# Spread products of the maxima, split inputs stored by GpSimd, values stored by tokens: a transformer layer on one Trainium2 core

## The chip, the cores and the metric

The kernel runs on one core of a Trainium2 chip. The core has a matrix engine (TensorE, "PE"), a vector engine (VectorE, "DVE"), a scalar engine (ScalarE, "ACT"), a general engine (GpSimd, "POOL") and a sync engine ("SP") which here only issues transfers. Each engine works through its own list of instructions in order; semaphores hold an instruction until its inputs are there and its output's memory is free. Transfers (DMAs) between DRAM and the on-chip memory are issued by SP, ACT and POOL into a queue of their own each and are carried by 16 DMA engines that all queues share. The metric is the time of one execution in device microseconds (us).

## The reference

One layer on 2048 tokens (S) of width 1024 (D), all in float32: attention with forget gates in 8 heads of 64, beside it a gated MLP over chunks of 128 positions, an output projection of both, and a feed-forward part.

```python
xn = rms_norm(x, mix_norm_g[l])
h = xn @ w_in[l]
q, k, v, f_logit, z = jnp.split(h, [D_ATTN, 2 * D_ATTN, 3 * D_ATTN, 3 * D_ATTN + N_ATTN_HEADS], axis=-1)
...
log_f = jax.nn.log_sigmoid(f_logit.astype(jnp.float32) + b_f[l].astype(jnp.float32))
attn = forgetting_attention(q, k, v, log_f)   # softmax(q.k/8 + c[t] - c[s], s <= t) @ v, c = cumsum(log_f)
sgu = spatial_gating(jax.nn.gelu(z, approximate=False), sgu_ln_g[l], sgu_ln_b[l], w_s[l], b_s[l])
merged = jnp.concatenate([rms_norm(attn, out_norm_g[l, :D_ATTN]), rms_norm(sgu, out_norm_g[l, D_ATTN:])], axis=-1)
x = x + merged @ w_out[l]
xn = rms_norm(x, ffn_norm_g[l])
gate, up = jnp.split(xn @ w_gate_up[l], 2, axis=-1)
x = x + (jax.nn.silu(gate) * up) @ w_down[l]
...
return rms_norm(x, final_norm_g)
```

## The kernel before, in words

**Split numbers.** PE multiplies in a shortened float format. Each operand is therefore split into a high part and a low part (names end in `h` and `l`: `xh`, `xl`, `wh`, `wl`), and a product takes three matmuls: high by high, high by low, low by high. L123 (ACT) makes a high part and L126 (DVE) a low one; both are helpers that all stages use.

**Projections (chunks).** The tokens go by in four chunks c = 0 to 3 of 512. For each chunk PE makes the logits of the forget gates (L526), then eight groups of 24 matmuls for queries and keys (L552: `which` = 0 is Q, 1 is K, `pr` is a pair of heads), then four groups of 24 for the values V (L447); chunk 0 has its V groups first. The split inputs of a chunk (`xh`, `xl`, two blocks of 128 features in each tile) are kept for later: `keep` (L266 to L269) writes them to the DRAM tensor `XS`, in the order [128, 4 token blocks, high/low, 8 feature blocks, 128 tokens], with four SP transfers of 256 KB for each pair, called after the stores of the low part of Q or K. Q and K go to DRAM as `QH`, `QL`, `KH`, `KL`, and the values (`v_close`, L447 to L461) as `VD`, in the order [head, token, 129], by ACT's queue or, for chunk 0 and the last two V groups of chunk 3, SP's.

**Maxima.** The softmax needs for each query the largest score over the keys. These are made from the high parts alone by extra matmuls: `one_max` (L354 to L363) multiplies 128 queries (a slice of tile `A`) with 512 keys (tile `D`) into a PSUM tile `mx_ps`, of which there are two, and DVE reduces it (L359, or L362 for the block on the diagonal). `max_stream` walks over the heads of a chunk and yields after each product; at the end of a head `turn` (L374 to L379) transposes the maxima and stores them (`md`). In the projections the maxima of chunk c−1 are run during chunk c (generator `early`): `between(n_early, ...)`, called after each group, takes the next `n_early` steps in one go (3, 6 and 7 for chunks 1, 2, 3, from the table `EB`), after one step of the forget gates (`gates_`, L310 to L350: the row of gates goes out to DRAM by ACT's queue, comes back by POOL's as `F`, and is then worked through by ACT, DVE and PE) and one step of loading the next chunk (`xg`). The remaining maxima are made during attention.

**Attention and z.** After the last V group come, interleaved on PE, the scores (L714, L715), the exponentials on ACT (L717), their split (L123, L126), the causal mask on POOL (L727) and the products with V (L747, L749, L752), and the z projection (L872) which reads the split inputs back from `XS`, one block of 128 tokens at a time: 32 tiles of 1 MB each. The first is loaded by SP into `wsth` and `wstl` (at the end of the projections); the other 31 (`xz`, two buffers) by POOL's queue (L865). Keys, queries and values (`D`, `C`, `A`, `B`, `V`) are loaded by SP.

**Output projection and feed-forward.** Each tile t of 128 tokens, once projected, goes through `out_done` (L1097 to L1116): the sum of squares on ACT, the reciprocal root `r3` in two steps (L172 on DVE, L174 on POOL), the scaling on DVE (L1106, `xn`, or `xb` for the last tile), and transposes on PE (L1113). It is a generator, and the caller takes one step of it between pieces of other work. The feed-forward part (L1614) starts on the result; its weights are added on POOL and DVE (L1303) and split.

**What sets the order.** The framework places each instruction by the order in which the code issues it and by its own estimate of when its inputs are ready; `behind(...)` (issue_after) holds everything inside until the named instructions have been placed. So the order on each engine is fixed when the program is built.

## Time and profile before

| | |
|---|---|
| median of 3 runs | 2403.47 us (2403.11 to 2408.91) |
| profiled execution | 2400.57 us |
| its span | 2398.9 us |
| DMA | 372.22 MB, mean 155 GB/s |
| HBM read, written | 249.15 MB, 120.98 MB |
| V stores by ACT's queue, chunks 1 to 3 (60 to 345 us) | 10 of 516 KB |
| stores of the split inputs by SP's queue (60 to 345 us) | 64 of 256 KB |

The profile was taken in one execution; times within it are counted from the start of the span. A row of the timeline names start, duration, engine, line, operation and tiles, and in brackets how long the engine stood idle just before and what it waited for. PE takes a matmul of 512 columns about every 0.23 us although each lasts 0.39, since they overlap. The stages are: projections from 0 to 345 us, attention with z from there to about 900, the output projection to about 1128, the feed-forward part to the end.

### The profile page before, as it was taken

To read this page: it belongs to the slowest core of one execution; us is meant where nothing else is said; L and a number is where in the kernel's file an instruction comes from. 1 tells how busy PE (TensorE), PEld (TensorE's weight loads), DVE (VectorE), ACT (ScalarE), POOL (GpSimd) and SP (SyncE) were. 2 spreads that over 40 slices of the span, in tenths; PEclk is the share of its full clock that TensorE was granted. 3 is DMA by queue.
4 is the path that set the end of the run, shared out by engine and by line. 5 is a ranking of instruction groups with operands and counts; after the bars stand their busy time and mean duration, and the time that the engine had idled before them with its cause. 6 is when DMAs were issued, how large, how long until landed. Compare 5 with 4: busy or idle time off the path is not lost. (4 is left out here: it accounts for less than half of the span.)

```text
span 2398.9 us, 31422 instructions
## 1 busy us (share of the span) xinstructions
PE 2344.1 (98%) x10582; PEld 1893.2 (79%) x10582; DVE 1668.5 (70%) x2736; ACT 1057.5 (44%) x1770; POOL 636.0 (27%) x704
## 2 busy tenths in 40 slices
PE   9999989999999999999999999999999999999998
PEld 7778767777777767877888888788888878888886
DVE  6658658888887676566656555965556587696888
ACT  5322127777777776444333332433333242332433
POOL 1000011222212232221323232422323244454431
PEclk9999999999999999999999999999999999999999
DMA  9856776555576655665333323433232344555453
GB/s 257 269 155 207 189 197 196 164 156 164 172 214 191 197 167 162 206 209 171 118 89 87 97 71 88 131 98 88 80 96 72 88 135 172 176 193 193 144 202 147
DMA packets 338632, 372.22 MB, mean 155 GB/s; under 512 B 22612, under 2 KB 259860, under 8 KB 332456
## 3 DMA queue, kind: packets, MB, share of 16 engines
q1 hardware_dynamic: 313672, 311.24, 42.9%
q0 software_dynamic: 7472, 43.06, 5.4%
q10 hardware_dynamic: 17328, 15.91, 2.3%
q8 instruction: 85, 1.39, 0.2%
q14 instruction: 75, 0.61, 0.1%
HBM read 249.15 MB, written 120.98 MB: 154 GB/s over the span
## 5 line engine op out<-in xcount | busy, mean ns | idle before, releaser
L123 ACT CAST wh<-raw 128x512 fp32r<-128x512 f32 (+2 forms) x492 | 302.1, 621 | 745.2 <-PE pp L1614 622.9
L126 DVE TENSOR_TENSOR wl<-raw,wh 128x512 fp32r<-128x512 f32 (+2 forms) x496 | 375.5, 767 | 83.8 <-ACT wh L123 83.3
L1614 PE MATMUL pp<-wl,wh 128*128 128x512 f32 x1056 | 325.3, 389 | 1.9 <-ACT u L1414 1.0
L1614 PE MATMUL pp<-wh,wh 128*128 128x512 f32 x1056 | 325.0, 389 | 0.0
L1303 POOL TENSOR_TENSOR raw<-raw 128x512 f32<-128x512 f32 (+1 forms) x124 | 171.1, 1381 | 524.6 <-DMA raw<-in_w_gu_dram 361.1
L126 DVE TENSOR_TENSOR Pl<-Pt,Ph 128x512 fp32r<-128x512 f32 (+1 forms) x320 | 195.9, 617 | 81.0 <-ACT Ph L123 76.3
L1614 PEld LDWEIGHTS pp<-wl,wh 128*128 128x128 f32 x1056 | 198.0, 188 | 43.7 <-ACT u L1414 1.4
L1614 PEld LDWEIGHTS pp<-wh,wh 128*128 128x128 f32 x1056 | 198.2, 188 | 41.1
L717 ACT ACTIVATE Pt<-mx_ps 128x512 f32<-128x512 f32 (+1 forms) x320 | 169.2, 533 | 124.9 <-PE mx_ps L715 119.5
L1614 PE MATMUL pp<-wl,wl 128*128 128x512 f32 x528 | 205.7, 390 | 1.0 <-DVE wl L126 0.9
L1614 PE MATMUL pp<-wh,wl 128*128 128x512 f32 x528 | 205.4, 389 | 0.0
L872 PE MATMUL z<-wh,xz 128*128 128x512 f32 x496 | 188.9, 396 | 0.0
L1303 DVE TENSOR_TENSOR raw<-raw,raw 128x512 f32<-128x512 f32 (+1 forms) x112 | 131.9, 1180 | 78.4 <-POOL raw L1303 74.9
L123 ACT CAST Ph<-Pt 128x512 fp32r<-128x512 f32 (+1 forms) x320 | 176.1, 556 | 20.8 <-PE tp L749 5.9
L359 DVE TENSOR_REDUCE mx<-mx_ps 128x1 f32<-128x512 f32 x192 | 129.8, 682 | 18.7 <-PE mx_ps L357 17.9
L747 PE MATMUL tp<-Ph,V 128*128 128x512 f32 (+1 forms) x320 | 119.1, 372 | 6.1 <-POOL Ph L727 4.5
L357 PE MATMUL mx_ps<-D,A 66*128 66x512 f32 (+2 forms) x320 | 116.7, 380 | 8.2 <-DVE mx L359 4.2
L752 PE MATMUL tp<-Pl,V 128*128 128x512 f32 (+1 forms) x320 | 119.4, 373 | 3.4 <-DVE Pl L126 2.7
L714 PE MATMUL mx_ps<-A,D 74*128 74x512 f32 (+1 forms) x320 | 119.6, 374 | 0.9 <-DMA A<-md 0.6
L715 PE MATMUL mx_ps<-B,C 128*128 128x512 f32 (+1 forms) x320 | 118.1, 369 | 0.0
L1614 PEld LDWEIGHTS pp<-wl,wl 128*128 128x128 f32 x528 | 99.1, 188 | 22.6 <-DVE wl L126 2.1
L1614 PEld LDWEIGHTS pp<-wh,wl 128*128 128x128 f32 x528 | 99.1, 188 | 20.6
(341 smaller groups left out, 5259.8 us busy)
## 6 DMA issues: line engine op xcount, KB each, us to landing
raw<-in_w_gu_dram SPq DMA_DIRECT2D x88, 512.0 KB
xz<-XS POOLq DMA_DIRECT2D x31, 1024.0 KB, 5.6
HD<-hT SPq DMA_DIRECT2D x44, 512.0 KB
D<-KH SPq DMA_DIRECT2D x112, 128.0 KB
XA<-xa SPq DMA_DIRECT2D x27, 512.0 KB
raw<-HD SPq DMA_DIRECT2D x24, 512.0 KB
XA<-xb SPq DMA_DIRECT2D x21, 512.0 KB
xa<-XA SPq DMA_DIRECT2D x20, 512.0 KB
```

Of the source, the lines that this page charges most:

```text
L123: return nc.scalar.copy(o, i) if eng is nc.scalar else eng.tensor_copy(o, i)
L126: return eng.tensor_tensor(o, i, f(h), ALU.subtract)
L357: nc.tensor.matmul(pm[:, 0:n], lhs, Dt[0 : lhs.shape[0], 0:n], start=True, stop=True)
L359: nc.vector.tensor_reduce(mx[:, a, s : s + 1], pm, AX.X, ALU.max)
L714: nc.tensor.matmul(st[:, off:], Dt[:, b * P : (b + 1) * P], A[:, off:], start=True, stop=False)
L715: nc.tensor.matmul(st[:, off:], C[:, b * P : (b + 1) * P], B[:, off:], start=False, stop=True)
L717: nc.scalar.activation(Pt[:, off:], st[:, off:], AF.Exp)
L747: nc.tensor.matmul(pv[:, off:], V[:, 0:P], Ph[:, off:], start=kb == 0, stop=False)
L752: nc.tensor.matmul(pv[:, off:], V[:, 0:P], Pl[:, off:], start=False, stop=kb == 4 * j + 3)
L872: nc.tensor.matmul(pz, xz[a][:, k, :], w[b][:, k, :], start=n == 0, stop=n == 3 * KT - 1)
L1303: (nc.vector if e == "v" else nc.gpsimd).tensor_tensor(o, a, b, op)
L1614: nc.tensor.matmul(pm, a[:, k, :], b[:, k, :], start=on is None and k == 0 and e == 0, stop=k == it.kh - 1 and e == 2, skip_group_check=n ...
```

## The change

1. `EB` for the last chunk is 12 in place of 10, so `n_early` there is 6 in place of 7. The steps of the maxima are no longer taken after a group: inside a group, ahead of the three matmuls of each feature block k, `maxima(n, k)` takes its even share of them, and holds the three matmuls behind the last maxima product that stood two calls earlier. So the maxima lie between the main products of all groups, Q, K and V.
2. `keep` stores each tile with one transfer of 512 KB on POOL's queue, with a dependency (`pace`) on the low part of Q or K of the same pair of heads; `XS` is laid out [128, high/low, 8, 512 tokens], so that a store writes runs of 4096 bytes and a load of 128 tokens reads runs of 512 bytes (before: the other way round, 512 and 8192).
3. `VD` is laid out [token, head, 129]: a store writes 4128 bytes in one run per token (before 516); a load still reads runs of 516 bytes.
4. The 31 `xz` loads are issued by SP in place of POOL; the load of the first two (`wsth`, `wstl`) reads the new layout.
5. In `out_done` the last two tiles (t = 14, 15) no longer stop between sum of squares, reciprocal root and scaling.

Numbers of instructions on PE, DVE and ACT stay; SP loses 64 stores and gains 31 loads; POOL gains 32 stores and loses 31 loads.

```diff
-EB = [1, 12, 12, 10]
+EB = [1, 12, 12, 12]
...
+    def pace(a, b):
+
+        tc.add_manual_dep(a.ins, b.ins.name, mybir.DependencyInfo(mybir.DependencyClass.Sync, mybir.DependencyReason.DATA),
+                          reason="pace")
...
-    XS = [T(dram, [P, 4, 2, KT, P], F32R, f"XS{c}") for c in range(NCH)]
+    XS = [T(dram, [P, 2, KT, CH], F32R, f"XS{c}") for c in range(NCH)]
...
-    VD = [T(dram, [H, CH, P + 1], F32R, f"VD{c}") for c in range(NCH)]
+    VD = [T(dram, [CH, H, P + 1], F32R, f"VD{c}") for c in range(NCH)]
...
-        def keep(self, i):
+        def keep(self, i, by):
             for a, t in enumerate((self.hi[i], self.lo[i])):
-                for m in range(2):
-                    s = ldr(XS[self.c][:, :, a, 2 * i + m, :], t[:, m].rearrange("p (t q) -> p t q", t=4))
+                pace(nc.gpsimd.dma_start(f(XS[self.c][:, a, 2 * i : 2 * i + 2, :]), f(t)), by)
...
-        nc.tensor.matmul(pm[:, 0:n], lhs, Dt[0 : lhs.shape[0], 0:n], start=True, stop=True)
+        last_mx.append(nc.tensor.matmul(pm[:, 0:n], lhs, Dt[0 : lhs.shape[0], 0:n], start=True, stop=True))
...
-    def between(n, *done):
+    def between(*done):
         with behind(*done):
             next(gates_, None)
             next(xg, None)
-        for _ in range(n):
+
+    def maxima(n, k):
+
+        marks.append(last_mx[-1:])
+        for _ in range((k + 1) * n // KT - k * n // KT):
             next(early, None)
+        return marks[0]
+
+    marks = deque([[], []], maxlen=3)
...
-        s = queue(xc.c if xc.c < NCH - 1 or tt < 2 else 0).dma_start(f(VD[xc.c][:, tt * P : (tt + 1) * P, :].rearrange("h p d -> p h d")), f(v))
+        s = queue(xc.c if xc.c < NCH - 1 or tt < 2 else 0).dma_start(f(VD[xc.c][tt * P : (tt + 1) * P]), f(v))
...
-                    for a, b in ((lh, rh), (lh, rl), (ll, rh)):
-                        mm = nc.tensor.matmul(pm, a, b, start=n == 0, stop=n == 3 * KT - 1)
-                        n += 1
+                    with behind(*maxima(n_early, k)):
+                        for a, b in ((lh, rh), (lh, rl), (ll, rh)):
+                            mm = nc.tensor.matmul(pm, a, b, start=n == 0, stop=n == 3 * KT - 1)
+                            n += 1
...
-                    with behind(s):
-                        xc.keep(pr)
+                    xc.keep(pr, b)
...
-                between(n_early, a, b, mm)
+                between(a, b, mm)
...
-            v_part(pm, xc, tt, range(KT))
+            for k in range(KT):
+                with behind(*maxima(n_early, k)):
+                    v_part(pm, xc, tt, [k])
...
-            between(n_early, a, b)
+            between(a, b)
...
-                nc.gpsimd.dma_start(f(xz.rearrange("p a k t -> p (a k t)")),
-                                    f(XS[q][:, cc].rearrange("p a k t -> p (a k t)")))
+                ldr(xz.rearrange("p a k t -> p (a k) t"),
+                    XS[q][:, :, :, cc * P : (cc + 1) * P].rearrange("p a k t -> p (a k) t"))
...
-        yield
+        if t < NB - 2:
+            yield
         r = rsqrt(pev, ss, 1.0 / D, "r3")
-        yield
+        if t < NB - 2:
+            yield
...
-        xz_in = [ldr(xz0[a], XS[0][:, 0, a]) for a in range(2)]
+        xz_in = [ldr(xz0[a], XS[0][:, a, :, 0:P]) for a in range(2)]
```

How this moves instructions is shown at three places.

PE, end of the third and start of the fourth V group of chunk 3, before (`mm` are the main products of V, `mx_ps` products for the maxima; numbers behind a name tell one tile from another):

```order
L447 MATMUL mm_3314<-wvh_273,xh_1714 128x512
L357 MATMUL mx_ps_3203<-D_3075,A_3050 128x512
L447 MATMUL mm_3314<-wvl_274,xh_1714 128x512
L447 MATMUL mm_3314<-wvh_273,xl_1718 128x512
L357 MATMUL mx_ps_3206<-D_3075,A_3050 128x512
L447 MATMUL mm_3314<-wvh_273,xh_1714 128x512
L447 MATMUL mm_3314<-wvl_274,xh_1714 128x512
L357 MATMUL mx_ps_3209<-D_3075,A_3050 128x512
L447 MATMUL mm_3314<-wvh_273,xl_1718 128x512
L447 MATMUL mm_3345<-wvh_273,xh_1711 128x512
L357 MATMUL mx_ps_3212<-D_3075,A_3050 128x512
L447 MATMUL mm_3345<-wvl_274,xh_1711 128x512
```

PE, end of the second V group and start of the third, after (line numbers of the changed file; L460 was L447, L363 was L357, L729 and L730 were L714 and L715):

```order
L363 MATMUL mx_ps_3243<-D_3104,A_3022 128x384
L460 MATMUL mm_3210<-wvh_273,xh_1698 128x512
L460 MATMUL mm_3210<-wvl_274,xh_1698 128x512
L460 MATMUL mm_3210<-wvh_273,xl_1702 128x512
L363 MATMUL mx_ps_3250<-D_3104,A_3022 128x512
L460 MATMUL mm_3210<-wvh_273,xh_1698 128x512
L460 MATMUL mm_3210<-wvl_274,xh_1698 128x512
L460 MATMUL mm_3210<-wvh_273,xl_1702 128x512
L460 MATMUL mm_3271<-wvh_273,xh_1695 128x512
L729 MATMUL mx_ps_3454<-A_3429,D_867_3414 128x512
L730 MATMUL mx_ps_3454<-B_3432,C_862_3409 128x512
L460 MATMUL mm_3271<-wvl_274,xh_1695 128x512
```

Before, a maximum stands behind every second matmul far into the fourth V group; after, the last maximum stands at the end of the second group, and the third and fourth hold first scores of attention in place of maxima. From that last maximum to the first z matmul there are 75 instructions; the first z stood directly behind the last V matmul and stands 18 instructions behind it now.

SP, end of the projections, before (`VD<-v` is the store of the third V group, `wsth` and `wstl` the first inputs of z, `KL` a store of a low part of K, `md` a store of maxima):

```order
L120 DMA C_865_3444<-KL_3_62_125 64x512
L120 DMA D_870_3449<-KH_3_46_109 64x512
L458 DMA VD_78_141<-v_3339 128x8x129
L120 DMA wsth_3429<-XS_7_70 128x1024
L120 DMA wstl_3430<-XS_7_70 128x1024
L120 DMA md_2_837_3273<-mr_3271 8x128
```

and after (L125 was L120, L471 was L458):

```order
L125 DMA KL_3_74_137<-ql_3139 128x512
L125 DMA md_2_818_3182<-mr_3180 8x128
L125 DMA D_870_3417<-KH_3_46_109 64x512
L125 DMA wsth_3397<-XS_7_70 128x8x128
L125 DMA wstl_3398<-XS_7_70 128x8x128
L125 DMA md_2_845_3287<-mr_3285 8x128
L471 DMA VD_78_141<-v_3307 128x1032
```

The two loads stood behind the store of V, now they stand ahead of it.

DVE, end of the output projection, before (`wl` and `wh` are weights of the feed-forward part, `r3a` the first step of the reciprocal root of the last tile, `xb` its scaling):

```order
L126 TENSOR_TENSOR wh_12290<-sg_3072_11568,wh_12290 128x2048
L126 TENSOR_TENSOR wl_12303<-raw_3201_12213,wh_12302 128x512
L126 TENSOR_TENSOR wl_12315<-raw_3199_12209,wh_12314 128x512
L126 TENSOR_TENSOR wl_12319<-raw_3201_12213,wh_12318 128x512
L126 TENSOR_TENSOR wl_12367<-raw_3200_12211,wh_12366 128x512
L1303 TENSOR_TENSOR raw_3199_12209<-raw_3200_12211,raw_3199_12209 128x512
L1303 TENSOR_TENSOR raw_3201_12213<-raw_12215,raw_3201_12213 128x512
L126 TENSOR_TENSOR wl_12373<-raw_12215,wh_12372 128x512
L172 TENSOR_SCALAR r3a_12402<-ss_3213_12286 128x1
L126 TENSOR_TENSOR wl_12438<-raw_3199_12209,wh_12437 128x512
L1106 SCALAR_TENSOR_TENSOR xb_12285<-xa_12055,r3r_12404,ffb_10109 128x1024
```

and after (L131 was L126, L177 was L172, L1123 was L1106, L1320 was L1303):

```order
L131 TENSOR_TENSOR wh_12279<-sg_3072_11536,wh_12279 128x2048
L177 TENSOR_SCALAR r3a_12272<-ss_3217_12270 128x1
L131 TENSOR_TENSOR wl_12292<-raw_3201_12181,wh_12291 128x512
L1123 SCALAR_TENSOR_TENSOR xb_12269<-xa_12023,r3r_12274,ffb_10077 128x1024
L131 TENSOR_TENSOR wl_12304<-raw_3199_12177,wh_12303 128x512
L131 TENSOR_TENSOR wl_12308<-raw_3201_12181,wh_12307 128x512
L131 TENSOR_TENSOR wl_12340<-raw_3200_12179,wh_12339 128x512
L1320 TENSOR_TENSOR raw_3199_12177<-raw_3200_12179,raw_3199_12177 128x512
L1320 TENSOR_TENSOR raw_3201_12181<-raw_12183,raw_3201_12181 128x512
L131 TENSOR_TENSOR wl_12346<-raw_12183,wh_12345 128x512
```

`r3a` stood behind seven weight instructions and stands directly behind the split of `sg` now; `xb` stands six rows earlier. On POOL, the second step `r3r` stood behind two adds of `raw` and stands ahead of them.

## The prediction, made before the changed kernel had run

> **What bounds the kernel now.** I read the page first, then busy time by stages, then TensorE's (PE) waits, then the timeline around the three places where it stands still.

> ```profile
> span 2398.9 us, 31422 instructions
> PE 2344.1 (98%) x10582; PEld 1893.2 (79%) x10582; DVE 1668.5 (70%) x2736; ACT 1057.5 (44%) x1770; POOL 636.0 (27%) x704
> ```

> PE works for 2344.1 of 2398.9 us. The change removes none of its matmuls, so only PE's idle 54.8 us and the time lost to a lowered clock can be won. The next view gives busy time by stage (columns: window, length, then busy us and instruction count by engine, then granted clock, DMA share, GB/s).

> ```profile
> core 0: us, PE busy (x) PEld busy (x) DVE busy (x) ACT busy (x) POOL busy (x), PEclk, DMA share, GB/s
> 95.00:345.00 250.00, 242.25 (x1092) 191.96 (x1091) 169.98 (x474) 60.56 (x86) 7.94 (x17) 0.99 0.71 195
> 345.00:360.00 15.00, 10.16 (x35) 7.47 (x34) 3.80 (x10) 5.34 (x12) 3.31 (x10) 0.77 0.73 183
> 360.00:620.00 260.00, 256.38 (x1214) 200.33 (x1214) 216.92 (x430) 190.39 (x337) 58.34 (x134) 1.00 0.57 170
> 620.00:885.00 265.00, 259.15 (x1234) 200.42 (x1233) 204.67 (x396) 208.88 (x387) 66.90 (x147) 1.00 0.60 185
> 1128.00:1136.00 8.00, 4.74 (x26) 3.77 (x25) 5.51 (x7) 2.83 (x5) 2.23 (x3) 1.00 0.49 186
> 1136.00:2399.00 1263.00, 1245.14 (x5483) 1027.90 (x5481) 860.41 (x1101) 427.41 (x686) 431.79 (x291) 1.00 0.39 122
> ```

> Length less busy time is PE's idle time: 7.75 us in chunks 1 to 3 of the projections, 4.84 us in the 15 us where these give way to attention, 3.62 and 5.85 us in the two halves of attention, 3.26 us where the output projection gives way to the feed-forward part, and 17.86 us in that part, which the change doesn't touch. Finer windows find the first two, and the clock:

> ```profile
> 98.00:126.00 28.00, 25.65 (x118) 20.45 (x117) 22.90 (x67) 14.12 (x20) 0.11 (x1) 1.00 0.95 281
> 176.00:186.00 10.00, 9.56 (x43) 7.29 (x42) 8.59 (x23) 5.99 (x9) 0.11 (x1) 1.00 0.63 192
> 264.00:275.00 11.00, 8.46 (x39) 6.64 (x38) 8.04 (x20) 4.20 (x7) 0.65 (x1) 1.00 0.58 170
> 325.00:335.00 10.00, 7.58 (x30) 5.62 (x29) 3.07 (x7) 2.18 (x3) 0.14 (x1) 0.93 1.08 229
> 335.00:345.00 10.00, 10.00 (x43) 8.07 (x42) 6.55 (x20) 0.69 (x1) 0.00 (x0) 0.90 0.57 122
> 345.00:355.00 10.00, 5.16 (x16) 3.74 (x15) 2.23 (x7) 3.38 (x8) 0.54 (x2) 0.78 0.76 167
> 355.00:365.00 10.00, 10.00 (x43) 7.42 (x42) 6.53 (x12) 5.66 (x10) 2.77 (x8) 0.88 0.85 278
> ```

> Four places hold all of the first 7.75 us: 2.35 + 0.44 + 2.54 + 2.42. Ten times what the clock lacks of 1.00 is the time lost to it in a 10-us row: 0.7 + 1.0 = 1.7 us around 335, 2.2 + 1.2 = 3.4 us behind 345. So at most 7.75 + 1.7 + 4.84 + 3.4 + 3.26 = 20.95 us can be won at the places that the change is near, outside of attention. What PE waits for there (us, times, longest):

> ```profile
> PE mx_ps L357 <- DVE mx L359: 4.2, 3, 2.5
> PE tp L331 <- DVE v L327: 2.6, 1, 2.6
> PE z L872 <- DMA wsth<-XS: 4.3, 1, 4.3
> PE tp L1113 <- DVE xb L1106: 3.3, 1, 3.3
> ```

> **The change part by part.**

> *Maxima spread between the main products.* No instruction is added on PE or VectorE (DVE); the order changes. A product for the maxima needs one of two banks, which DVE frees with its reduction (L359, L362). Where several stand close together in PE's order and DVE is late, PE stops. That is so in the V groups of chunk 3:

> ```profile
> 331.41 0.39 PE L447 MATMUL mm<-wvh,xl 128*128 128x512 f32 x1
> 333.01 0.50 PE L357 MATMUL mx_ps<-D,A 66*128 66x512 f32 x1 [1.21 <-DVE mx L359]
> 333.35 0.45 PE L447 MATMUL mm<-wvh,xh 128*128 128x512 f32 x1
> 333.59 0.63 PE L447 MATMUL mm<-wvl,xh 128*128 128x512 f32 x1
> 334.02 0.63 PE L357 MATMUL mx_ps<-D,A 66*128 66x512 f32 x1
> ```

> ```profile
> DVE v L456 <- DMA VD<-v: 7.5, 1, 7.5
> ```

> DVE stood 7.5 us at v's low part, because v's buffer was still being stored, and the maxima behind it stood with it. In the new order the dense stretch is gone and the third and fourth V group hold no maximum at all, so a late DVE holds nobody there. I count the places at 98, 176 and 325, with the clock that fell at the last, as won: 2.35 + 0.44 + 2.42 + 1.7 = 6.9 us. At 264 something else is late:

> ```profile
> 268.76 0.23 DVE L321 TENSOR_SCALAR v<-v 128x128 f32<-128x128 f32 x1 [2.96 <-issue]
> ```

> DVE idles for 2.96 us ahead of the forget gates, whose row comes back from DRAM behind the V stores; these become shorter (below), but the chain stays. I take half of 2.54, 1.3 us, between 0 and 2.54. Part sum −8.2 us, bounds 0 and −9.45.

> What it may cost: every main product now stays behind maxima of two calls before, so PE can't run ahead of a full DVE. How full DVE is:

> ```profile
> 185.00:215.00 30.00, 30.00 (x143) 24.61 (x142) 27.98 (x73) 11.45 (x16) 0.00 (x0) 1.00 0.83 250
> ```

> 93% in chunk 2, and PE lost nothing here; the row at 176 lost 0.44 us beside DVE at 86%. At worst each of about six such groups waits for one reduction of about 0.7 us: 4 us; at best 0. Six times 0.44 would be 2.6; I take 1.5 us, nearer to the row of 185 to 215.

> *The inputs' split tiles stored by GpSimd (POOL), V by tokens.* Sixty-four stores of 256 KB leave SP's queue, 32 of 512 KB enter POOL's. POOL is busy for 7.94 of 250 us here, so its issues have room; each waits for a low part, and behind it stand the next chunk's forget row and r, due a chunk later. SP's queue is what is relieved: D, KL and QL no longer stand behind stores. I give this no term of its own: it is why the first part's gains should hold. Bounds −1 and +2 us, the +2 if r or the forget row behind a held store comes late.

> *The first z loads.* At the seam PE goes from V directly to z, whose first input lands late:

> ```profile
> 345.13 0.39 PE L447 MATMUL mm<-wvh,xl 128*128 128x512 f32 x1
> 349.86 0.47 PE L872 MATMUL z<-wh,wsth 128*128 128x512 f32 x1 [4.34 <-DMA wsth<-XS]
> ```

> ```profile
> 340.34 0.39 SPq L458 DMA_DIRECT2D VD<-v  x1
> 340.83 0.53 SPq L120 DMA_DIRECT2D wsth<-XS  x1
> 341.41 1.12 SPq L120 DMA_DIRECT2D wstl<-XS  x1
> ```

> wsth leaves 0.5 us behind the V store for which SP held still, and lands 9 us after its issue (340.83 to 349.86). In the new order both loads stand ahead of that store; wstl's memory is free once the last maximum is done, which is 75 PE instructions, about 75 × 0.23 = 17 us (the step of PE's rows above), ahead of the first z. 9 us fit into 17. The wait and the clock behind it go: 4.84 + 3.4 = −8.2 us. What is late next: 18 scores and P-times-V products now stand ahead of the first z, and the later of these wait for exp, split and mask of scores that stand some 2 us ahead of them; I give back 1 us, between 0 and 3. Part sum −7.2 us, bounds 0 and −8.2.

> *Two steps less in the last tiles' norm.*

> ```profile
> 1124.49 2.49 DVE L126 TENSOR_TENSOR wl<-raw,wh 128x512 fp32r<-128x512 f32 x4
> 1131.04 0.14 DVE L172 TENSOR_SCALAR r3a<-ss 128x1 f32<-128x1 f32 x1
> 1132.23 1.28 DVE L1106 SCALAR_TENSOR_TENSOR xb<-xa,r3r,ffb 128x1024 f32<-128x1024 f32 x1 [0.44 <-POOL r3r L174]
> 1125.91 3.46 POOL L1303 TENSOR_TENSOR raw<-raw 128x512 f32<-128x512 f32 x2 [9.86 <-DVE wl L126]
> ```

> r3a moves ahead of the four splits at 1124.49 and r3r ahead of POOL's two adds, so xb can start near 1127 instead of 1132.23, and PE's 3.26 us go. In turn the adds start about 2 us later, and the last weight split behind them comes later by that, some 0.7 us more than its cover: −3.3 + 0.7 = −2.6 us, bounds −3.3 and 0.

> *The 31 later z loads go from POOL's queue to SP's*, in 512-byte pieces.

> ```profile
> xz<-XS POOLq DMA_DIRECT2D x31, 1024.0 KB, 5.6
> POOL xz L865 <- PE z L872: 111.1, 17, 18.8
> SPq L120 <- PE mx_ps L357: 110.2, 44, 11.6
> ```

> Now POOL stands 111.1 us for a free xz buffer, with masks behind it; then SP does, with keys and queries behind it. PE's attention loses 9.47 us now, of which some could go with POOL's hold; against it SP's loads come later. Neither shows as a price: I take 0, between −3 and +8 (and the rival below).

> **The sum.** The profiled execution took 2400.57 us (span 2398.9 and 1.7 around it). −8.2 + 1.5 − 7.2 − 2.6 + 0 = −16.5, so 2384.1; the runs shown have their median at 2403.47, 2.9 above, which would give 2387. I forecast 2385.

> [...] The row at 333.59 shows the half clock (0.42 from start to start in place of 0.23) behind two waits of 1.2 us, while the idle 3.26 us at 1128 left the clock at 1.00. [...] The rows speak for the waits, so I keep −16.5.

> **Rivals.**
> 1. *DVE becomes the bound of the spread maxima.* PE is tied to DVE's pace and chunk 1 to 3 give back what they win. For it: 93% in the row from 185; against it: no idle PE in that row. Then −7.2 − 2.6 = −9.8: 2391. Chance 14%.
> 2. *The seam's wait only changes its name*: z's first input is there, but masks or V are late behind SP's queue. For it: the 2 us of cover worked out above. Then −6.7 − 2.6 = −9.3: 2391. Chance 8%. Both 1 and 2: −2.6, 2398, no measurable change; 9%.
> 3. *Slower: SP holds z back.* Eight of the 31 xz loads have only some 40 PE instructions, 40 × 0.23 = 9.2 us, between the release of their buffer and first use; 5.6 us are the landing, so some 3.6 us are left. SP's waits in attention are long (110.2 us in 44, up to 11.6); where one stands ahead of such a load, z stops PE. It decides from 3.6 us of delay; 4 us beyond that at the eight tiles cost 32 us: 2400.6 − 16.5 + 32 = 2416. Against it: POOL reached 17 of its xz loads early, so the buffer, not the queue, set their time. Chance 12%.

> **How the numbers follow.** A measurement of this kernel can tell about 0.3%, 7 us, from no change. My forecast, 57%, covers 2376 to 2389. Faster: 57 + most of 14 and 8 = 76%. Within: 9 and the rest = 12%. Slower: 12%. The range must leave out no more than 2 in 10: below, all 20.95 us won and a little in attention, 2375; above, the double rival with its spread, 2402; rival 3 stays outside.

> **What would show it.** Right: no PE wait for wsth and a clock near 1.00 from 345 to 365; windows from 325 to 345 without idle PE; xb ahead of PE at the seam to the feed-forward part; PE idle in attention still near 9.5 us. Wrong: new waits of mx_ps for DVE mx in chunks 2 and 3 (rival 1), of tp or mx_ps L714 behind 345 (rival 2), of z for xz between 360 and 885 with idle time there well over 9.5 us (rival 3).

## The result and the profile after

The changed kernel takes 2388.7 us (median of 4 runs, 2382.4 to 2391.42) against 2403.48 (2403.11 to 2408.91): a ratio of 0.993, 95% interval 0.9904 to 0.9955. Its profiled execution took 2382.40 us, 18.2 less than the one of before. It is the fastest of its four; the medians lie 14.8 us apart. The forecast was 2385. Of all runs below, one, of e5_values, took 2882.31 us at a mean granted clock of 0.752; e5's median and ratio below are those of its other five.

The page of the changed kernel and its busy time by the same windows as before (columns as there):

```profile
span 2380.7 us, 31420 instructions
PE 2337.5 (98%) x10582; PEld 1893.8 (80%) x10582; DVE 1671.2 (70%) x2736; ACT 1056.2 (44%) x1770; POOL 633.6 (27%) x705
```

```profile
95.00:345.00 250.00, 244.36 (x1103) 195.07 (x1102) 172.88 (x475) 64.71 (x97) 21.94 (x48) 0.99 0.58 198
345.00:360.00 15.00, 15.00 (x71) 11.62 (x70) 12.07 (x20) 8.67 (x17) 1.85 (x7) 1.00 0.55 165
360.00:620.00 260.00, 255.19 (x1215) 201.69 (x1214) 216.63 (x433) 192.91 (x338) 48.90 (x114) 1.00 0.63 172
620.00:885.00 265.00, 258.60 (x1234) 200.37 (x1233) 206.51 (x395) 206.02 (x386) 58.32 (x135) 1.00 0.70 195
```

The seam to attention (345 to 360) is full, at full clock, where 4.84 us were idle and the clock stood at 0.77. The two windows of attention idle 4.81 and 6.40 us, against 3.62 and 5.85, but they hold later work now; from the first z matmul to the last PE idles 7.37 us (before 7.78). But the projections (95 to 345) still idle 5.64 us of the 7.75, and not where they did: the windows at 98 to 126 and 264 to 275 have 28.00 of 28 and 10.93 of 11 us busy now, while PE stands still here:

```profile
315.18 0.39 PE L460 MATMUL mm<-wvh,xl 128*128 128x512 f32 x1
319.13 1.19 PE L363 MATMUL mx_ps<-D,A 66*128 66x512 f32 x2 [3.56 <-DMA D<-KH]
320.12 0.63 PE L460 MATMUL mm<-wvh,xh 128*128 128x512 f32 x1
321.91 0.80 PE L363 MATMUL mx_ps<-D,A 66*128 66x512 f32 x1 [1.16 <-DVE mx L365]
```

3.56 us for a tile `D` of keys, then 1.16 us for DVE, and the clock falls with it (0.63 us for a matmul in place of 0.39). The next table follows the same instructions of PE through both profiled executions (start in us; "600th" is the 600th matmul of the feed-forward part).

| PE instruction | before | after | gained up to here |
|---|---|---|---|
| first matmul of chunk 1 | 85.72 | 84.13 | 1.6 |
| of chunk 2 | 166.49 | 161.88 | 4.6 |
| of chunk 3 | 253.34 | 248.52 | 4.8 |
| last Q or K matmul | 315.06 | 307.95 | 7.1 |
| last V matmul | 345.13 | 341.01 | 4.1 |
| last z matmul | 867.30 | 853.71 | 13.6 |
| last of the output projection | 1116.41 | 1099.23 | 17.2 |
| 600th | 1258.93 | 1238.21 | 20.7 |
| end of the span | 2398.86 | 2380.69 | 18.2 |

The V groups of chunk 3, where the prediction looked for most of its gain in the projections, gave back 3.0 us of 7.1. The first 1.6 us aren't clear of chance: eight kernels of this document give PE the same work in the same order up to chunk 1, and reach it at 83.72 to 87.59 us in their profiled executions.

### The profile page after: what moved, and what is told of

It is laid out like the page before. It is cut to its first block, busy times and chain, and to the rows that moved or that the text cites. A ratio compares the mean times of both kernels' runs of the same rounds, so it can differ in the third digit from the quotient of the medians.

```text
span 2380.7 us, 31420 instructions
## 1 busy us (share of the span) xinstructions
PE 2337.5 (98%) x10582; PEld 1893.8 (80%) x10582; DVE 1671.2 (70%) x2736; ACT 1056.2 (44%) x1770; POOL 633.6 (27%) x705
## 3 DMA queue, kind: packets, MB, share of 16 engines
q8 instruction: 85, 1.39, 0.2%
## 5 line engine op out<-in xcount | busy, mean ns | idle before, releaser
L131 DVE TENSOR_TENSOR wl<-raw,wh 128x512 fp32r<-128x512 f32 (+2 forms) x496 | 375.9, 767 | 81.5 <-ACT wh L128 81.0
L1320 POOL TENSOR_TENSOR raw<-raw 128x512 f32<-128x512 f32 (+1 forms) x124 | 171.2, 1382 | 518.3 <-DMA raw<-in_w_gu_dram 354.5
L131 DVE TENSOR_TENSOR Pl<-Pt,Ph 128x512 fp32r<-128x512 f32 (+1 forms) x320 | 195.6, 616 | 71.1 <-ACT Ph L128 69.8
L1320 DVE TENSOR_TENSOR raw<-raw,raw 128x512 f32<-128x512 f32 (+1 forms) x112 | 133.9, 1198 | 81.0 <-POOL raw L1320 77.7
L742 POOL TENSOR_SCALAR_AFFINE_SELECT Ph<-Ph 128x128 fp32r<-128x128 f32 x128 | 52.3, 408 | 350.4 <-DVE Pl L131 267.2
L363 PE MATMUL mx_ps<-D,A 66*128 66x512 f32 (+2 forms) x320 | 119.6, 376 | 5.1 <-DMA D<-KH 3.6
L729 PE MATMUL mx_ps<-A,D 74*128 74x512 f32 (+1 forms) x320 | 118.9, 372 | 0.8 <-ACT Pt L732 0.5
L730 PE MATMUL mx_ps<-B,C 128*128 128x512 f32 (+1 forms) x320 | 117.2, 367 | 0.0
## 6 DMA issues: line engine op xcount, KB each, us to landing
xz<-XS SPq DMA_DIRECT2D x31, 1024.0 KB
```

Source lines behind the costliest of these rows:

```text
L131: return eng.tensor_tensor(o, i, f(h), ALU.subtract)
L363: last_mx.append(nc.tensor.matmul(pm[:, 0:n], lhs, Dt[0 : lhs.shape[0], 0:n], start=True, stop=True))
L729: nc.tensor.matmul(st[:, off:], Dt[:, b * P : (b + 1) * P], A[:, off:], start=True, stop=False)
L730: nc.tensor.matmul(st[:, off:], C[:, b * P : (b + 1) * P], B[:, off:], start=False, stop=True)
L1320: (nc.vector if e == "v" else nc.gpsimd).tensor_tensor(o, a, b, op)
```

## Experiments

Ratios are against runs of the kernel before on the same chip, with 95% intervals. The kernels were timed on several chips, on which the kernel before has medians of 2402.16 to 2405.68 us, so they are compared by ratio rather than by median.

| run | what it is | median us | ratio |
|---|---|---|---|
| (the change) | all parts | 2388.70 | 0.9930 [0.9904, 0.9955] |
| e1_spread | maxima spread, nothing else | 2413.36 | 1.0036 [1.0023, 1.0049] |
| e2_io | storage, nothing else | 2382.51 | 0.9910 [0.9895, 0.9925] |
| e3_out | shorter last norm, nothing else | 2400.95 | 0.9985 [0.9970, 1.0000] |
| e4_eb8 | the change, maxima end earlier | 2380.68 | 0.9897 [0.9881, 0.9913] |
| e5_values | V by tokens, nothing else | 2389.54 | 0.9931 [0.9909, 0.9953] |
| e6_inputs | split inputs' part, nothing else | 2395.04 | 0.9959 [0.9945, 0.9973] |
| e7_inputs_sp | storage, but stores of inputs by SP | 2389.30 | 0.9929 [0.9904, 0.9954] |
| e8_no_spread | the change without spreading | 2378.92 | 0.9890 [0.9867, 0.9914] |
| e9_late_keys | the change, attention's keys later | 2381.51 | 0.9911 [0.9895, 0.9926] |
| e10_no_hold | the change without the hold | 2376.96 | 0.9895 [0.9880, 0.9911] |
| e11_spread_values | spreading and V by tokens | 2407.97 | 1.0021 [1.0010, 1.0032] |
| e12_bursts_of_8 | e8 with bursts of 8 | 2381.23 | 0.9912 [0.9895, 0.9930] |

### The parts alone

**e1_spread**: item 1 of the change alone.

```diff
-                    for a, b in ((lh, rh), (lh, rl), (ll, rh)):
+                    with behind(*maxima(n_early, k)):
+                        for a, b in ((lh, rh), (lh, rl), (ll, rh)):
...
-                between(n_early, a, b, mm)
+                between(a, b, mm)
```

> Only the maxima are spread between the main products (EB 12 in the last chunk, shares inside the groups); inputs, V, z loads and the last norms stay as before. Theory A (the order of the maxima makes most of the gain of the projections and of the seam): -10 to -14 us against before, a ratio of 0.994 to 0.996; PE's wait for wsth gone, no idle PE at 98 to 126 and 264 to 275; the start of chunk 2 stays late, since SP's queue is still full of stores. Theory B (relief of SP's queue makes the gain): -3 us or less, PE still waits for D<-KH and wsth.

It is slower, by 0.36%. Theory A, which was the prediction's, falls; theory B is nearer, with a loss in place of its small gain. PE's waits in the first 620 us (us, times, longest), and two rows of SP's timeline:

```profile
PE mx_ps L359 <- DMA D<-AUG: 11.4, 2, 7.8
PE mx_ps L726 <- DVE mx L364: 4.2, 1, 4.2
```

```profile
311.83 0.51 SPq L120 DMA_DIRECT2D C<-KH  x1
...
327.30 0.25 SPq L120 DMA_DIRECT2D D<-AUG  x1
```

PE stands 7.8 us at one maximum of chunk 3 whose `D` isn't loaded. SP issued nothing but attention's first keys, values, queries and their maxima from 311.83 on, and then, at 327.30, the missing part of `D`. The last V matmul comes at 361.69, 16.6 us later than before.

**e2_io**: items 2, 3 and 4 alone (`XS`, `VD`, the queues).

```diff
-    XS = [T(dram, [P, 4, 2, KT, P], F32R, f"XS{c}") for c in range(NCH)]
+    XS = [T(dram, [P, 2, KT, CH], F32R, f"XS{c}") for c in range(NCH)]
...
-    VD = [T(dram, [H, CH, P + 1], F32R, f"VD{c}") for c in range(NCH)]
+    VD = [T(dram, [CH, H, P + 1], F32R, f"VD{c}") for c in range(NCH)]
```

> Only the storage changes: split inputs stored by GpSimd in 512 KB pieces, V by tokens, the 31 z loads by SP; maxima in bursts after the groups, as before. Theory A: -2 to -5 us (chunk 0's 1.9 us and its clock, shorter V stores), the wait for wsth stays above 3 us. Theory B: -10 us or more, and the stalls of the projections are gone without the spreading.

Theory B's number, and more: 0.991, at least as good as the whole change. PE's waits from 250 to 345 us, the stretch in which the kernel before stood still at 266, 329 and 331, are now all of these (two rows):

```profile
PE mx_ps L717 <- ACT Pt L720: 0.3, 1, 0.3
PE mx_ps L361 <- DVE mx L363: 0.3, 1, 0.3
```

The last V matmul comes at 336.75 (before 345.13, the change 341.01). The stalls go without any spreading.

**e3_out**: item 5 alone, the two `yield`s.

> Only the two steps of the last two tiles' norm are taken out. Both theories: PE's 3.3 us wait for xb at the seam to the feed-forward part goes, the 1.1 us behind it may go or come back in the weights: -2.5 to -4.5 us, a ratio of 0.998 to 0.999. If the waits of the feed-forward part take it back: 0.

Within its range, 0.9985; the interval just reaches 1.0. The trace is clear: of PE's waits from 1100 to 1140 the 3.3 us for `xb` are gone, and these are left:

```profile
PE tp L1115 <- DVE xn L1108: 0.5, 1, 0.5
PE pp L1616 <- ACT u L1416: 0.2, 1, 0.2
```

### Which part of the storage

**e5_values** (the new `VD` alone) and **e6_inputs** (the new `XS`, GpSimd's stores and SP's z loads alone).

> Only V is stored by tokens (a store writes 4128 bytes in a run); all else as before. The storage change alone gave 0.991. Theory Q (SP's queue of 64 more stores makes keys, maxima's D and wsth late): 0 to -3 us, PE's wait for wsth stays. Theory V (V stores in 516-byte pieces land late, hold DVE's memset, and behind it the maxima, and wsth): -8 us or more, no idle PE at 325 to 335.

> Only the split inputs' part: XS laid out anew, stored by GpSimd, 31 z loads by SP; V, maxima and last norms as before. Theory Q: -12 us or more, wsth's wait gone. Theory V: -8 us or less, DVE still held 5 us or more by V's store in chunk 3.

In e5 theory V holds: no PE idle from 325 to 335, and no wait for `wsth`. In e6 each theory has one half right: the wait for `wsth` is gone, and DVE is still held. V by tokens, a change of one layout, gives 0.69% by itself; the split inputs' part 0.41%. A V store and the DVE row that waits for it, in the kernel before and then in e5 (start, length, idle time before):

```profile
322.76 0.38 ACTq L458 DMA_DIRECT2D VD<-v  x1
331.48 0.23 DVE L456 SCALAR_TENSOR_TENSOR v<-mm,r,v 128x8 fp32r<-128x8 f32 x1 [7.51 <-DMA VD<-v]
```

```profile
318.11 0.33 ACTq L458 DMA_DIRECT2D VD<-v  x1
322.47 0.07 DVE L454 MEMSET v<- 128x8 f32 x1 [3.15 <-DMA VD<-v]
```

The same 516 KB kept the buffer for 8.7 us, and now 4.4 us. DVE's wait, behind which the maxima's reductions stand, falls from 7.5 to 3.2 us, and PE's stalls at 329 and 331 go. With the split inputs' part alone DVE still waits 7.1 us there, PE 3.1 us at 331, and the half clock with it; the last V matmul is at 347.78, later than before.

```profile
DVE v L460 <- DMA VD<-v: 7.1, 1, 7.1
```

The two parts act at different places. From the first matmul of chunk 1 to that of chunk 3 it takes 167.62 us before, 167.30 in e5 and 164.88 in e6: here the inputs' part counts. From there to the last V matmul it takes 91.79 us before, 85.21 in e5 and 95.93 in e6: here V's layout counts. The larger gain of the inputs' part lies at the seam: from the last V to the last z matmul it takes 513.2 us in e6 and 519.7 in e5, against 522.2 before. In e6 the 18 instructions stand ahead of the first z, in e5 z still follows V directly and waits 1.8 us.

**e7_inputs_sp**: e2 with the 32 stores back in SP's queue.

```diff
-                pace(nc.gpsimd.dma_start(f(XS[self.c][:, a, 2 * i : 2 * i + 2, :]), f(t)), by)
+                ldr(XS[self.c][:, a, 2 * i : 2 * i + 2, :], t)
```

> The whole storage change, but the 32 stores of the split inputs stay in SP's queue, each behind the store of the low part, as before. If it is the queue that counts (SP's list waits and holds keys and maxima behind the stores): 8 us or more of the 21 us are lost again, 2390 us or above. If it is the pieces (fewer, longer ones, less DMA time): 2386 us or below.

2389.3 us lies between the two bounds, and its interval lies over e2's, so the times alone decide nothing. By the trace the projections are nearly as good as in e2 (last V at 336.08), and the seam is what is lost (522.1 us from last V to last z, e2 512.3), with these waits:

```profile
PE z L876 <- DMA xz<-XS: 4.0, 2, 2.7
PE z L876 <- DMA wstl<-XS: 1.6, 1, 1.6
```

The longer and fewer stores are worth 1.6 us in the projections (165.67 us from chunk 1 to chunk 3, e5 167.30, e2 164.89) and nothing from there to the last V matmul (85.13, 85.21, 85.32). GpSimd's queue serves the first z loads, which stand earlier in SP's list: in e2 `wsth` leaves at 328.35, ahead of the V store at 334.68, in e7 at 331.75, behind the one at 331.30.

### Why spreading costs, and three ways to mend it

**e8_no_spread**: the change without item 1.

> The changed kernel without the spreading: storage change and the shorter last norm, maxima in bursts of 3, 6 and 7 after the groups. If spreading gives nothing beside the storage change: -21 - 3 = 2377 to 2381 us, that is 7 us or more below the changed kernel's 2388.7, since its stall and half clock at 315 to 325 go. If spreading helps once the queue is relieved: above 2386 us.

2378.9 us; all its runs (2377.7 to 2381.0) lie below all of the changed kernel's. By the ratios, 0.9890 and 0.9930, spreading costs 0.4% in the changed kernel, some 10 us; the two intervals overlap by 0.001. In the traces the price lies in chunk 3: from its first matmul to the last V matmul it takes 92.49 us in the changed kernel and 85.21 here, while chunks 1 and 2 take 164.39 and 164.96.

**e4_eb8**: eight maxima in each group of chunk 3, so that the last stands ahead of the last K matmul.

```diff
-EB = [1, 12, 12, 12]
+EB = [1, 12, 12, 8]
```

> The changed kernel with 8 in place of 12 in the last entry of EB: eight maxima in a group of chunk 3, so that they end with the last K group and no V group holds any. Theory A (the 3.6 and 1.2 us that PE stood still at 315 to 322 of the changed kernel, and the half clock behind, come from maxima whose D loads stand in SP's list behind attention's first keys, and from a DVE held by v's store): PE idle from 300 to 330 falls by 4 us or more and the clock there stays at 1.00: -6 to -9 us against the changed kernel, near 2375 in the profile. Theory B (the stall moves with the maxima, DVE becomes the bound of chunk 3's K groups): new waits of mx_ps for DVE mx between 255 and 310, gain under 3 us or a loss.

Theory A's number: 0.9897 against the change's 0.9930 is 0.33%, or 8 us, and the profiled execution took 2375.88. The half clock at 318 and every wait over 0.5 us between 62 and 330 us are gone; the last V matmul is at 333.47. No new wait for DVE.

**e9_late_keys** asks where the late `D` comes from. SP's list in the changed kernel:

```profile
296.87 0.35 SPq L125 DMA_DIRECT2D KL<-ql  x1
297.32 0.48 SPq L125 DMA_DIRECT2D C<-KH  x1
...
313.92 0.44 SPq L125 DMA_DIRECT2D A<-md  x1
314.46 0.27 SPq L125 DMA_DIRECT2D md<-mr  x1
314.83 0.45 SPq L125 DMA_DIRECT2D D<-KH  x1
315.33 0.43 SPq L125 DMA_DIRECT2D D<-AUG  x1
```

From 297.32 to 313.92 SP issues only attention's first loads; the `D` on which PE stands from 315.6 is issued at 314.83.

```diff
-        with behind(k_low[1]):
+        with behind(k_low[3]):
```

> The changed kernel, with attention's first keys and queries held in SP's list behind the last low part of K in place of the second (k_low[3] for k_low[1]), so that the last D loads for the maxima stand ahead of them. If the 3.6 us at 315 come from D loads late in SP's list: no wait of mx_ps for D<-KH over 1 us between 300 and 330, clock 1.00 there, the last V matmul at 332 to 335 in place of 341.0; the first z may then wait up to 5 us. If they come from DVE held by v's store: 1 to 2 us less at most, last V at 339 or later.

PE's wait for `D` is gone, and so is the half clock. Between 250 and 345 us these are the longest that are left:

```profile
PE z L887 <- ACT Pt L732: 1.8, 1, 1.8
PE tp L380 <- DVE mh L131: 1.7, 1, 1.7
```

The last V matmul, at 336.90, comes 4 us earlier, but 2 us later than expected: 1.7 us stand in the second row, and this execution came to chunk 1 at 85.59 us, 1.5 later than the changed kernel's. The whole gains 0.2% by the ratios (0.9911 against 0.9930), with intervals that lie over each other. So the place in SP's list made the load late (PE's list changes a little too: the first z stands directly behind V again); what that is worth in the whole isn't clear of noise.

**e10_no_hold**: maxima placed as in the change, but nothing held behind them.

```diff
-        return marks[0]
+        return ()
```

> The changed kernel with the maxima spread as before, but the main products not held behind earlier maxima (maxima() returns nothing to wait for). If the hold is what makes PE stand at late D loads: last V 4 us or more earlier than 341.0, 2380 to 2384 us. If the placing alone does it: last V within 2 us of 341, 2386 to 2391 us; maxima that slip to the end of V then stand close together and wait for DVE.

2377.0 us, below the expected range; its ratio of 0.9895 can't be told from e8's 0.9890 and e4's 0.9897. In PE's list the last maximum of chunk 3 now stands 32 instructions ahead of the last V matmul in place of 56: with the hold gone, the scheduler itself puts the maxima with a late `D` later, and V's products go ahead of them. SP issues the `D` of the stall no earlier than in the changed kernel (314.83 there):

```profile
316.00 0.27 SPq L125 DMA_DIRECT2D md<-mr  x1
316.37 0.45 SPq L125 DMA_DIRECT2D D<-KH  x1
```

PE's waits from 250 to 345:

```profile
PE mx_ps L363 <- DVE mx L368: 0.3, 1, 0.3
PE mx_ps L729 <- ACT Pt L732: 0.3, 1, 0.3
```

**e11_spread_values** and **e12_bursts_of_8** close two gaps.

> Spreading and V by tokens, with the split inputs' stores and z loads as before (64 stores in SP's queue). Spreading alone was +0.36%, V by tokens alone -0.69%. If spreading hurts through SP's queue (PE now meets each D load sooner, and these stand behind stores): it loses 4 us or more against V by tokens alone, 2395 us or above, with mx_ps waiting for D loads. If it hurt only through V's stores: 2388 to 2392 us.

0.9931 with V by tokens becomes 1.0021 once the spreading is added: PE waits 7.1 us, from 317.9 on, and the last V matmul moves from 336.20 to 350.36.

```profile
PE mx_ps L359 <- DMA D<-AUG: 7.1, 1, 7.1
```

So it isn't only V's stores through which spreading hurts. The `D` leaves SP at 320.98, and from 304.03 to there SP issues attention's first loads, as in e1, and no store of the split inputs.

> The kernel without spreading (storage change and shorter norm) with bursts of 8 in place of 7 in chunk 3. If maxima that end sooner help whatever their form: 2375 to 2379 us. If 7 were fine already: 2377 to 2382 us, no difference that can be told from e8's 2378.9.

2381.2, against e8's 2378.9: the intervals lie over each other. A gain from ending sooner in bursts isn't shown; e4's gain fits the stall that spreading had made.

## Why the prediction held, and where it didn't

| term | predicted | in the profiled executions |
|---|---|---|
| projections, to the last V matmul | −8.2 + 1.5 = −6.7 | −4.1 |
| seam and attention, to the last z matmul | −7.2 + 0 | −9.5 |
| last z to the end of the output projection | 0 | −3.6 |
| from there to the 600th matmul | −2.6 | −3.5 |
| the rest | 0 | +2.6 |
| sum | −16.5 | −18.2 |

*The time* was right, and inside its range (the right column is one execution of each kernel, and 1.6 of its first 4.1 us lie ahead of chunk 1); *the reason for the first term was wrong*. The failing step is the one that put the projections' gain on the spreading ("I count the places at 98, 176 and 325, with the clock that fell at the last, as won") and gave the storage "no term of its own". The runs show the reverse: storage alone wins 0.9%, spreading alone loses 0.36%. The prediction read the stall at 331 rightly as DVE held by V's store, with the row of 7.5 us before its eyes; it then removed those who stood behind the wait in place of the wait. V by tokens shortens the wait itself (7.5 to 3.2 us in e5). That the sum came so near is luck: the storage is worth 0.9%, about 22 us, where the sum had only the 7.2 of the seam for it, and the spreading costs some 10 us where 6.7 were to be won. The two errors cancel.

*A wait at the wrong place.* The prediction lists 2.6 us for `DVE v` among the waits at its places. That wait stands in chunk 0, at 58 us, which the change leaves alone, and is still there after; PE's 2.54 us near 267 are one of the three waits for `DVE mx` in the row above it.

*"A late DVE holds nobody there"* was true of the third and fourth V group. The second one holds eight maxima, and there PE stood 3.56 us for a load and 1.16 us for DVE, which had itself waited 3.36 us for V's store. Rival 1 named the tie between PE and the maxima, but with DVE's pace as its limit; the limit was mainly SP's list. e10 shows that the tie (the hold) is what makes it a cost, e9 that the place in SP's list makes the load late. The 1.5 us put down for the tie don't show in chunks 1 and 2; in chunk 3 the tied maxima cost 7.3.

*The clock at 335* came back at 318, for 6.8 us in place of 3.4.

*The forget gates' row at 264*: half of 2.54 us was taken; all of it went (2.54 to 0.07). e5 alone removes that stall, e6 alone doesn't (3.4 us there): it was V's stores ahead of the row on ACT's queue, as the prediction had it, with too small a share. POOL can fetch the row 3.95 us after ACT sends it before (260.04 to 263.99), and 1.8 us after in e5 (257.69 to 259.46).

*The seam*: rightly sized (the window from 345 is full, and the 1 us held back didn't come due), with a cause that e6 and e7 confirm: SP's list puts the first z loads ahead of the V store because the inputs' stores are gone from it. Rival 2 did not come.

*The last norm*: −3.5 against −2.6; the 0.7 us held back for the weights didn't come due.

*Rival 3*, SP holding back z, did come in small: z waits for `xz` 2.0 us in two places near 361 and 377, behind the first loads, where nothing showed before.

```profile
PE z L887 <- DMA xz<-XS: 2.0, 2, 1.4
```

It is far from the 32 us of that rival; the tight tiles later on all came in time.

*The 3.6 us between z and the end of the output projection* were not forecast. The half clock accounts for 1.7 of them: the kernel before had 3.4 us of it at 907 (0.94 in the window from 885 to 912), the changed one none there (1.00). That needn't be the change's doing: e4, e9 and e10, which do the same work there as the changed kernel, have 3.4 us of half clock in this stretch, at 871, 890 and 887. Another 1.2 us are idle time in several small waits (7.74 us to 6.52); the rest stays open. The +2.6 behind the 600th matmul hold 1.7 us of half clock at 1957 (last section) and 1.1 us more idle time (16.75 us to 17.88).

## What to carry to other kernels

Where an engine waits because another is held, shorten what holds that one (here a store in 516-byte pieces, which kept its buffer for 8.7 us, against 4.4 in 4128-byte runs) before moving work out of its way. Tying the main work to the order of side work, so that it stays spread, made a late input of the side work a stall of the main (3.56 us for one `D`); a scheduler left free put the late ones back. And a change that comes out as forecast can still owe it to another of its parts: only the parts alone showed that one of them was a loss.

## What the runs showed of the hardware

**Short pieces.** ACT's queue carries, among others, ten V stores and the high parts of Q and K. The pages have the whole queue as packets, MB and share of the 16 engines' span, with V in 516-byte pieces (before) and in 4128-byte runs (after):

```profile
q10 hardware_dynamic: 17328, 15.91, 2.3%
```

```profile
q10 hardware_dynamic: 8368, 15.91, 1.8%
```

The 8960 packets that are gone are V's: ten stores of 516 KB are 10240 pieces of 516 bytes before and 1280 of 4128 after. By the packets of these sizes in the two traces, the same 5.28 MB took 406.9 us of the engines' time together before and 211.9 after, so the engines' time for them was halved. So was the time from issue to free buffer (8.7 to 4.4 us in the kernel before and e5), beside other transfers.

```profile
1953.66:1957.07 3.41, 1.22 (x6) 0.71 (x5) 3.41 (x4) 0.00 (x0) 2.96 (x2) 1.00 0.78 192
1957.07:1960.49 3.42, 3.42 (x10) 2.67 (x9) 3.34 (x6) 1.65 (x3) 0.37 (x1) 0.50 0.74 274
```

```profile
1971.95:1975.36 3.41, 2.69 (x12) 1.88 (x10) 3.41 (x4) 0.00 (x0) 2.78 (x2) 1.00 0.58 163
1975.36:1978.78 3.42, 1.95 (x8) 1.61 (x9) 3.42 (x3) 0.20 (x1) 2.56 (x2) 1.00 0.98 299
```

```profile
330.15:333.56 3.41, 1.93 (x7) 1.35 (x8) 2.08 (x6) 0.00 (x0) 0.00 (x0) 1.00 0.89 273
333.56:336.97 3.41, 3.41 (x9) 2.66 (x8) 2.06 (x3) 0.00 (x0) 0.00 (x0) 0.50 0.58 159
```

Near 1955 and 1975 both kernels idle 2.2 us. In the changed kernel these lie in one step, and 3.4 us at 0.50 follow; in the kernel before they fall as 0.72 and 1.47 us into two, and no half clock follows. The idle 3.26 us at 1128, which the prediction set beside the waits at 333, fall as 1.87 and 1.39 into two steps as well, while the step ahead of 333.56 held 1.48 and was followed by half clock. In the 14 traces of this case, from 100 us on, each of the 38 steps at full clock in which PE idled 1.9 us or more was followed by half clock, and of the thousands with less than 1.4 us only one (1.06 us, e8 at 489); between 1.4 and 1.9 us both occur. So 2.2 idle us of 3.41 were enough in the step at 1953.66, and 1.48 in the one at 330.15. The prediction was right to take the half clock at 335 for a price of the waits ahead of it.

The clock also fits the spread of the changed kernel's runs, whose span and mean clock go together (2380.7 us at 0.996, 2385.0 at 0.995, 2388.9 at 0.994, 2389.7 at 0.992): 0.4% of clock is 9.5 us, as much as they lie apart. That the stall at 315 is what lowers the clock more in some runs than in others wasn't shown, since only one execution has a trace; of the kernels without it, e10 stood at 0.997 to 0.999, e4 at 0.995 to 0.997.
